# A SwiGLU kernel on one core: four rows per partition to a store, and sixty consecutive rows to each partition

## The chip, the core and the metric

The kernel runs on one core of a Trainium2 chip. The core has several engines with a queue of instructions each: VectorE (DVE), ScalarE (ACT), GpSimd (POOL) and SyncE (SP) are used here, TensorE is not. Sixteen DMA engines move data between DRAM and the on-chip memory, which has 128 partitions. Transfers are issued by SP, ACT or POOL; each of the three has a queue of its own on the DMA engines, and a transfer is done when its semaphore has been raised. The metric is the device time of one execution in microseconds (us). In the profile the transfers that SP issues are queue q1, those of ACT q10 and those of POOL q0.

## The reference

`x` is 8192 x 8192 in float32 (268 MB). Its left half is `a` and its right half `b`; the output is 8192 x 4096 (134 MB):

```python
a, b = np.split(x, 2, axis=-1)
silu_b = b / (1 + np.exp(-b))
return a * silu_b
```

Every element of `x` is read once and every element of the output is written once, 402.65 MB in all. One row of `x` is 32 KiB and one row of the output is 16 KiB.

## The kernel before

The rows are dealt out in 33 tiles. The first and the last tile have one row per partition (128 rows), the 31 between them two rows per partition (256 rows). Partition p of a two-row tile holds two neighbouring rows, so that a load moves 64 KiB in one piece to each partition and a store 32 KiB in one piece; the 128 pieces of a tile stand one behind the other in DRAM (L36 to L38, `in_dram`).

There are three buffers, the slots, of 64 KiB per partition, and tile i uses slot i modulo 3. For each tile `load` (L50) issues the load on SP. `swiglu` (L57) computes in the slot: ACT replaces `b` by silu(b) in place (L62), and DVE multiplies it by `a` and packs the products into the front of the same slot (L64). `store` (L73) sends that front part to DRAM. The two rows of a tile are one ACTIVATE and one multiplication of 128 x 8192 elements; tiles 1 and 31 are done in two pieces of one row (128 x 4096), and the first and last tile in two halves of a row (128 x 2048).

The program order is written out by hand at L83 to L97: three loads ahead, then for each tile compute, store, and the load that is to use the same slot. That load waits for the store (SP, L51), the store waits for the multiplication, the multiplication for the activation, and the activation for the load. Other waits between them are left out (`follows_from_others`), since they follow from these. Which engine issues a store is settled at L74 to L76: ACT, except for two stores in the middle of the kernel on POOL and the last three on SP. An engine's queue is worked off in order, so an instruction that waits holds up those behind it on the same engine.

Of the kernel before, what the change touches and what calls it, by code (L numbers as in the profile page):

```python
# [1 line left out]

# [4 lines left out]

_SILU = mybir.ActivationFunctionType.Silu


@with_exitstack
def kernel(
    ctx: ExitStack,
    tc: tile.TileContext,
    x: bass.AP,
    out: bass.AP,
):

    nc = tc.nc  # L20
    N, M = x.shape
    half = M // 2
    P = nc.NUM_PARTITIONS
    BUFS = 3

    rows = [1] + [2] * (N // P // 2 - 1) + [1]
    first = [sum(rows[:i]) * P for i in range(len(rows))]
    last = len(rows) - 1

    pool = ctx.enter_context(tc.tile_pool(name="sbuf", bufs=1))  # L30
    ctx.enter_context(tc.manual_schedule())
    slots = [pool.tile([P, 2 * M], x.dtype, name=f"slot{s}") for s in range(BUFS)]
    loads, gates, prods, stores = ([[] for _ in rows] for _ in range(4))
    newest = {}

    def in_dram(t, i, width):  # L36

        return bass.AP(t.tensor, first[i] * width, [[rows[i] * width, P], [1, rows[i] * width]])  # L38

    def follows_from_others(inst, i, current, earlier):  # L40


        targets = [t for kind in current for t in kind[i]]
        targets += [t for kind in earlier for j in range(i % BUFS, i, BUFS) for t in kind[j]]
        for t in targets:
            if t is not newest.get(inst.ins.engine):
                tc.declare_no_dep(inst.ins, t.ins, reason="ordered by the other waits")
        newest[inst.ins.engine] = inst

    def load(i):  # L50
        inst = nc.sync.dma_start(  # L51
            out=slots[i % BUFS][:, : rows[i] * M], in_=in_dram(x, i, M)
        )
        follows_from_others(inst, i, [], [loads, gates, prods])
        loads[i].append(inst)

    def swiglu(i, k0, k1, c0=0, cw=half):  # L57
        view = slots[i % BUFS].rearrange("p (k s c) -> p k s c", k=2, s=2)
        a = view[:, k0:k1, 0, c0 : c0 + cw]
        b = view[:, k0:k1, 1, c0 : c0 + cw]  # L60
        o = slots[i % BUFS][:, : 2 * half].rearrange("p (k c) -> p k c", k=2)
        gate = nc.scalar.activation(out=b, in_=b, func=_SILU)  # L62
        follows_from_others(gate, i, [], [loads, gates, prods, stores])
        prod = nc.vector.tensor_mul(out=o[:, k0:k1, c0 : c0 + cw], in0=a, in1=b)  # L64
        follows_from_others(prod, i, [loads], [loads, gates, prods, stores])
        gates[i].append(gate)
        prods[i].append(prod)

    def by_halves(i):
        for c0 in range(0, half, half // 2):  # L70
            swiglu(i, 0, 1, c0, half // 2)

    def store(i):  # L73
        eng = nc.scalar if i < last - 2 else nc.sync  # L74
        if i % 2 and last // 2 <= i < last // 2 + 4:
            eng = nc.gpsimd  # L76
        inst = eng.dma_start(  # L77
            out=in_dram(out, i, half), in_=slots[i % BUFS][:, : rows[i] * half]
        )
        follows_from_others(inst, i, [loads, gates], [loads, gates, prods, stores])  # L80
        stores[i].append(inst)

    for i in range(BUFS):  # L83
        load(i)
    for i in range(last):
        if i == 0:
            by_halves(i)
        elif i in (1, last - 1):
            swiglu(i, 0, 1)
            swiglu(i, 1, 2)  # L90
        else:
            swiglu(i, 0, rows[i])
        store(i)
        if i + BUFS <= last:
            load(i + BUFS)
    by_halves(last)
    store(last)  # L97


# [1 line left out]
_INS = ['x']  # L101
_OUTS = [((8192, 4096), 'float32')]


# [23 lines left out]
```

## Time and profile before

| | |
|---|---|
| median of three timed runs | 935.07 us (934.86 to 935.34) |
| profiled execution, first to last instruction | 933.16 us (the page rounds to 933.2) |
| around the span, against the median | 1.9 us |
| DVE busy | 278.7 us (30%), 37 instructions |
| ACT busy | 226.8 us (24%), 38 instructions |
| DMA packets | 9505, of which 1056 small ones that raise semaphores |
| HBM read and written | 268.44 MB and 134.22 MB, 431 GB/s over the span |
| loads, issue to landing (median) | 37.7 us |
| stores from ACT, issue to landing (median) | 33.5 us |

The profile is of one execution. Its page gives the busy time of each engine, the span in 40 slices with the busy share of the DMA engines in tenths, and the DMA queues with packets, bytes and the share of sixteen DMA engines that their packets took. The groups show instructions of one line and shape: count, busy time, mean duration in ns, the idle time before them and what ended it. A packet is one contiguous piece that one DMA engine moves: here the piece of one partition. The trace also keeps a record of each packet: its queue, size, start and duration.

### The profile page before, as it was taken

What the parts mean: (1) busy time and instruction counts of PE and PEld (TensorE: products, weight loads), DVE (VectorE), ACT (ScalarE), POOL (GpSimd) and SP (SyncE); (2) the same over time, 40 slices, a digit from 0 to 9 for tenths busy, and PEclk for the clock granted to TensorE, in tenths of its full rate; (3) what the DMA queues carried; (4) which work ended last, traced back from release to release, by engine and by line L of the source; (5) the groups of instructions that cost most, each with busy time, mean ns of one, the idle gap of its engine ahead of it and who ended that gap; (6) DMA issues with size and microseconds to landing.
All of it is one profiled execution on the core that took longest, in us unless ns stands there. A gap on an engine that the chain in (4) does not pass through costs nothing.

```text
span 933.2 us, 220 instructions
## 1 busy us (share of the span) xinstructions
DVE 278.7 (30%) x37; ACT 226.8 (24%) x38; POOL 1.4 (0%) x6
## 2 busy tenths in 40 slices
DVE  1312333123331233312333113332133321333242
ACT  2331133311333203332033320233202332023330
POOL 0000000000000000000000000000000000000000
DMA  9999999999999999999999999999999999999998
GB/s 405 405 449 431 423 451 444 409 444 433 444 427 434 442 410 448 428 433 442 434 421 441 445 417 444 428 454 427 420 457 405 449 427 428 448 445 409 427 444 388
DMA packets 9505, 402.67 MB, mean 432 GB/s; under 512 B 1056, under 2 KB 1056, under 8 KB 1056
## 3 DMA queue, kind: packets, MB, share of 16 engines
q1 hardware_dynamic: 5184, 278.92, 69.1%
q10 hardware_dynamic: 4032, 115.35, 28.6%
q0 software_dynamic: 288, 8.39, 2.1%
q14 instruction: 1, 0.01, 0.0%
HBM read 268.44 MB, written 134.22 MB: 431 GB/s over the span
## 4 chain that ended last, share of the span: by engine, by line
DMA 72%; DVE 11%; ACT 8%; issue 6%; another core or an unknown queue 1%; DVEq 0%; POOL 0%; SPq 0%; ACTq 0%; POOLq 0%
DMA slot<-in_x_dram 40%; DMA out_dram<-slot 32%; DVE slot L64 11%; ACT slot L62 8%; DVEq L123 0%; POOL out_dram L77 0%; SPq L51 0%; ACTq L77 0%; DVEq L64 0%; POOLq L123 0%
## 5 line engine op out<-in xcount | busy, mean ns | idle before, releaser
L64 DVE TENSOR_TENSOR slot<-slot 128x8192 f32<-128x8192 f32 (+2 forms) x37 | 278.7, 7539 | 636.7 <-ACT slot L62 636.5
L62 ACT ACTIVATE slot<-slot 128x8192 f32<-128x8192 f32 (+2 forms) x37 | 225.6, 6107 | 684.3 <-DMA slot<-in_x_dram 684.3
L77 POOL DMA_DIRECT2D out_dram<-slot x2 | 1.2, 600 | 568.9 <-DVE slot L64 568.9
L62 ACT ACT_TABLE_LOAD x1 | 1.3, 1283 | 0.7 <-PEq L112 0.7
L112 POOL MEMSET const-bfloat16-1.0<- 128x1 bf16 x1 | 0.1, 102 | 0.0
L112 POOL MEMSET const-float32-0.0<- 128x1 f32 x1 | 0.1, 99 | 0.2 <-issue 0.2
L112 POOL MEMSET const-float32-1.0<- 128x1 f32 x1 | 0.1, 99 | 0.0
L112 POOL MEMSET const-uint8-127<- 128x1 uint8 x1 | 0.1, 99 | 0.0
## 6 DMA issues: line engine op xcount, KB each, us to landing
out_dram<-slot ACTq DMA_DIRECT2D x27, 4096.0 KB, 33.5
slot<-in_x_dram SPq DMA_DIRECT2D x2, 4096.0 KB, 13.6
out_dram<-slot POOLq DMA_DIRECT2D x2, 4096.0 KB, 34.4
out_dram<-slot SPq DMA_DIRECT2D x2, 4096.0 KB, 20.4
out_dram<-slot ACTq DMA_DIRECT2D x1, 2048.0 KB, 28.1
out_dram<-slot SPq DMA_DIRECT2D x1, 2048.0 KB, 16.8
slot<-in_x_dram SPq DMA_DIRECT2D x31, 37.7
```

The source lines that it names most:

```text
L62: gate = nc.scalar.activation(out=b, in_=b, func=_SILU)
L64: prod = nc.vector.tensor_mul(out=o[:, k0:k1, c0 : c0 + cw], in0=a, in1=b)
L77: inst = eng.dma_start(out=in_dram(out, i, half), in_=slots[i % BUFS][:, : rows[i] * half])
L112: nc = _bacc.Bacc("TRN2", target_bir_lowering=False, num_devices=1)
```

## The change

The row order in DRAM and the use of the slots both change. The computation on each element does not.

The first 384 rows stay as they were: a one-row tile and a two-row tile. The last 128 rows stay a one-row tile too. The 7680 rows between them are divided among the partitions in 128 runs of 60 consecutive rows, and each partition works through its own run in 15 groups of four rows. `PITCH` is the distance of 60 rows between neighbouring partitions, which is 1,920 KiB in `x` and 960 KiB in the output.

A group of four rows is loaded by two loads of two rows, 64 KiB per partition each. The first, called A here, goes to a main slot (`mains`, two of the three slots, taken in turn), the second, called B, to the side slot (`side`, the third). A's rows are computed in place as before, two rows in one instruction of each engine. B's rows are computed one row at a time, and DVE writes their products not into the side slot but behind A's products in the main slot. The four rows of products then fill the main slot, 64 KiB per partition, and one store, called S, sends them. S of group g waits for the last product of the group.

The load A of group g+1 goes to the other main slot and waits for the store that frees it, that of group g-1. The load B of group g+1 waits for the last product of group g only, since the side slot is never stored from. On SP the order is A(g+1), B(g+1), A(g+2) and so on. The stores of groups 7, 8 and 9 are issued by POOL, the stores of group 14 and of the last one-row tile by SP, all others by ACT. The load of the last one-row tile stands behind B(14) on SP and waits for the store of group 13.

There are 33 loads as before, and 18 stores instead of 33. The core of the diff:

```diff
-    BUFS = 3
-
-    rows = [1] + [2] * (N // P // 2 - 1) + [1]
-    first = [sum(rows[:i]) * P for i in range(len(rows))]
-    last = len(rows) - 1
+    groups = (N // P - 4) // 4
+    PITCH = 4 * groups
...
-    slots = [pool.tile([P, 2 * M], x.dtype, name=f"slot{s}") for s in range(BUFS)]
+    slots = [pool.tile([P, 2 * M], x.dtype, name=f"slot{s}") for s in range(3)]
+    side, mains = slots[0], slots[1:]
...
+    def in_dram(t, start, step, rows, width):
+        return bass.AP(t.tensor, start * width, [[step * width, P], [1, rows * width]])
...
+    def swiglu(src, row, rows, dst, at, *needed, pieces=1):
+
+        view = src.rearrange("p (k s c) -> p k s c", k=2, s=2)
+        packed = dst.rearrange("p (k c) -> p k c", k=4)
+        last = None
+        for c0 in range(0, half, half // pieces):
+            cols = slice(c0, c0 + half // pieces)
+            a = view[:, row : row + rows, 0, cols]
+            b = view[:, row : row + rows, 1, cols]
+            gate = after(nc.scalar.activation(out=b, in_=b, func=_SILU), *needed)
+            last = after(
+                nc.vector.tensor_mul(out=packed[:, at : at + rows, cols], in0=a, in1=b), gate
+            )
+        return last
+
+    first = load(side, 0, 1, 1)
+    second = load(mains[0], P, 2, 2)
+    lead = [load(mains[1], 3 * P, PITCH, 2)]
+    base = 3 * P
+    firsts = {0: lead[0]}
+
+    done = swiglu(side, 0, 1, side, 0, first, pieces=2)
+    stored = store(nc.scalar, side, 0, 1, 1, done)
+    free_side = stored
+
+    def group(g):
+        return base + 4 * (g if PITCH != 4 else g * P)
+
+    seconds = {0: load(side, group(0) + 2, PITCH, 2, free_side)}
+    swiglu(mains[0], 0, 1, mains[0], 0, second)
+    done = swiglu(mains[0], 1, 1, mains[0], 1, second)
+    free = {0: store(nc.scalar, mains[0], P, 2, 2, done), 1: None}
+    last = None
+    for g in range(groups):
+        m = (g + 1) % 2
+        other = 1 - m
+        if g + 1 < groups:
+            firsts[g + 1] = load(mains[other], group(g + 1), PITCH, 2, free[other])
+        else:
+            last = load(mains[other], N - P, 1, 1, free[other])
+        swiglu(mains[m], 0, 2, mains[m], 0, firsts[g])
+        for k in range(2):
+            done = swiglu(side, k, 1, mains[m], 2 + k, seconds[g])
+        eng = nc.scalar if g + 1 < groups else nc.sync
+        if groups // 2 <= g < groups // 2 + 3:
+            eng = nc.gpsimd
+        free[m] = store(eng, mains[m], group(g), PITCH, 4, done)
+        if g + 1 < groups:
+            seconds[g + 1] = load(side, group(g + 1) + 2, PITCH, 2, done)
+    done = swiglu(mains[1 - m], 0, 1, mains[1 - m], 0, last, pieces=2)
+    store(nc.sync, mains[1 - m], N - P, 1, 1, done)
```

`load` issues on SP as before, `store` on the engine that it is given. The helper `after` takes the place of `follows_from_others`: it leaves to each instruction only the waits that are passed to it by name.

More of the change, by code (lines that the diff above doesn't have):

```diff
@@ L23 @@
     P = nc.NUM_PARTITIONS
-    BUFS = 3
-    rows = [1] + [2] * (N // P // 2 - 1) + [1]
-    first = [sum(rows[:i]) * P for i in range(len(rows))]
-    last = len(rows) - 1
+    groups = (N // P - 4) // 4
+    PITCH = 4 * groups
     pool = ctx.enter_context(tc.tile_pool(name="sbuf", bufs=1))
     ctx.enter_context(tc.manual_schedule())
-    slots = [pool.tile([P, 2 * M], x.dtype, name=f"slot{s}") for s in range(BUFS)]
-    loads, gates, prods, stores = ([[] for _ in rows] for _ in range(4))
+    slots = [pool.tile([P, 2 * M], x.dtype, name=f"slot{s}") for s in range(3)]
@@ L34, with after @@
+    side, mains = slots[0], slots[1:]
     newest = {}
[L36 to L46, printed above, removed]
+    def after(inst, *needed):
+        for t in (t for ts in everything for t in ts):
+            if t not in needed and t is not inst and t is not newest.get(inst.ins.engine):
@@ L47, in follows_from_others, with load @@
                 tc.declare_no_dep(inst.ins, t.ins, reason="ordered by the other waits")
         newest[inst.ins.engine] = inst
-    def load(i):
+        history.append(inst)
+        return inst
+    def in_dram(t, start, step, rows, width):
+        return bass.AP(t.tensor, start * width, [[step * width, P], [1, rows * width]])
+    history = []
+    everything = [history]
+    def load(slot, start, step, rows, *needed):
         inst = nc.sync.dma_start(
-            out=slots[i % BUFS][:, : rows[i] * M], in_=in_dram(x, i, M)
+            out=slot[:, : rows * M], in_=in_dram(x, start, step, rows, M)
@@ L53, in load @@
         )
[L54 to L75, printed above, removed]
-            eng = nc.gpsimd
[L77 to L97, printed above, removed]
+        return after(inst, *needed)
+    def store(eng, slot, start, step, rows, *needed):
+        inst = eng.dma_start(
+            out=in_dram(out, start, step, rows, half), in_=slot[:, : rows * half]
+        )
+        return after(inst, *needed)
@@ new lines, in swiglu @@
+    def swiglu(src, row, rows, dst, at, *needed, pieces=1):
[9 more added lines that the diff above has]
+                nc.vector.tensor_mul(out=packed[:, at : at + rows, cols], in0=a, in1=b), gate
+            )
+        return last
```

## The prediction

> **What bounds the kernel now.** I read the page's slices and DMA queues first, then the groups by form, the stretches at the end, and the waits of the queue of SP.
>
> ```profile
> DMA  9999999999999999999999999999999999999998
> GB/s 405 405 449 431 423 451 444 409 444 433 444 427 434 442 410 448 428 433 442 434 421 441 445 417 444 428 454 427 420 457 405 449 427 428 448 445 409 427 444 388
> DMA packets 9505, 402.67 MB, mean 432 GB/s; under 512 B 1056, under 2 KB 1056, under 8 KB 1056
> q1 hardware_dynamic: 5184, 278.92, 69.1%
> q10 hardware_dynamic: 4032, 115.35, 28.6%
> q0 software_dynamic: 288, 8.39, 2.1%
> ```
>
> The three queues add up to 99.8% of 16 DMA engines for the whole span: transfers bound the kernel from start to end, and no hole is left to fill. The engines are far behind:
>
> ```profile
> L64 DVE TENSOR_TENSOR slot<-slot 128x8192 f32<-128x8192 f32 x29 | 252.1, 8692 | 588.7 <-ACT slot L62 588.7
> L62 ACT ACTIVATE slot<-slot 128x8192 f32<-128x8192 f32 x29 | 203.9, 7031 | 633.6 <-DMA slot<-in_x_dram 633.6
> L64 DVE TENSOR_TENSOR slot<-slot 128x4096 f32<-128x4096 f32 x4 | 17.7, 4426 | 33.2 <-ACT slot L62 32.9
> L62 ACT ACTIVATE slot<-slot 128x4096 f32<-128x4096 f32 x4 | 14.2, 3609 | 37.1 <-DMA slot<-in_x_dram 37.1
> ```
>
> They idle two thirds of the time, waiting for loads. So only two things can move the time: what the DMA engines need for the same bytes, and whether they ever run dry. The stretches of the end (busy time and count per engine, clock, DMA share, GB/s) and its timeline show how close that is:
>
> ```profile
> 850.00:890.00 40.00, 17.39 (x2) 8.24 (x2) 0.00 (x0) 1.00 1.00 433
> 890.00:900.00 10.00, 0.00 (x0) 1.59 (x1) 0.00 (x0) 1.00 1.03 446
> 900.00:910.00 10.00, 7.84 (x2) 7.41 (x4) 0.00 (x0) 1.00 1.02 442
> 910.00:920.00 10.00, 5.42 (x3) 1.84 (x2) 0.00 (x0) 1.00 0.98 423
> ```
> ```profile
> 893.38 22.40 SPq L77 DMA_DIRECT2D out_dram<-slot  x3
> 898.41 7.12 ACT L62 ACTIVATE slot<-slot 128x4096 f32<-128x4096 f32 x2 [18.28 <-DMA slot<-in_x_dram]
> 902.06 13.36 DVE L64 TENSOR_TENSOR slot<-slot 128x4096 f32<-128x4096 f32 x4 [13.21 <-ACT slot L62]
> ```
>
> The last two-row load lands at 898.4 and its rows are multiplied by about 911.0 (902.06 + 2 × 4.43, and small hops), when its store can go. In those 12.6 us the DMA still holds the last one-row load and the store issued at 893.38, 4.19 MB each, 9.7 us each: 19.4 us of work. That is why the share stays near 1.00 there. The reader should keep this pair, work in the queue against time to the next issue, for the change.
>
> **The price of bytes and packets.** The trace's packet records (per queue and size) give it: all but a few 65,536-byte packets took 2,418 ns, 32,768 bytes 1,213, 16,384 bytes 611. The line through them is 8 ns per packet and 27.2 GB/s per engine, 435 GB/s for sixteen; each transfer ends with a 4-byte packet of 9 ns on each engine. Check: per engine before, 402.65 MB / 16 at 27.2 GB/s is 925.2 us, 528 packets × 8 ns 4.2, 66 transfers × 9 ns 0.6: 930.0, against first packet at 1.7 and last end at 931.9. So the records leave under a microsecond of idling.
>
> The records of one engine also show the order: a packet of one queue, then one of the other, whatever their sizes (S64 A32 S64 A32, 3.63 us a pair).
>
> **The change, part by part.**
>
> *Fewer, larger store packets.* Stores per partition: before 1 + 31 + 1 transfers, one packet each, 33 × 8 = 264 packets per DMA engine. After: 18 transfers (1 row, 2 rows, fifteen of 4, 1 row), 144 packets. Saved: 120 × 8 ns = 0.96 us, and 15 final packets × 9 ns = 0.13 us. Loads keep 33 transfers and 264 packets. Sum -1.1 us, all on the path, because the DMA is the path. The Trainium skill (DMA: Bandwidth & Descriptors, Anatomy of one DMA) prices each transfer at 2.0 us plus its bytes, which read as a cost in series would make 15 transfers fewer worth -30 us; the DMA share of 1.00 above speaks against it, since the fixed part lies under other transfers.
>
> *Smaller compute pieces.* The side slot's rows go one at a time: 30 pairs at 3.61 and 4.43 us in place of 15 at 7.03 and 8.69. ACT +0.19 × 15 = 2.9 us, DVE +0.17 × 15 = 2.5 us. Cost 0: hidden by the transfers, as the idle columns show. After the side load lands, 3.61 + 2 × 4.43 = 12.5 us pass until the group's store may go (one-piece form: 15.7).
>
> *Waits in the loop.* Call a group's loads A (into a main slot) and B (into the side slot), 8.39 MB each, its store S, 8.39 MB. A group is 25.2 MB, 58.1 us of DMA. SP issues A(g+1) when S(g-1) has landed, then B(g+1) when group g is multiplied, which is also when S(g) is issued. So S(g) and B(g+1) start together, but B queues behind what is left of A(g+1), and the two queues take turns packet by packet. With A(g+1) started when B(g) ended, 19.4 us long, and 12.5 us of compute plus about 1.3 of landing and issue gone, 5 to 6 us of A (2 to 3 packets per engine) are left. S therefore finishes that many packets ahead of B: 5 to 7 us, against about 1.3 us that A(g+2) needs to be issued and start. The DMA stays full; cost 0 per group, cover 4 to 5 us. If that cover were gone, up to 1.3 us a group. ACT waits with each store for DVE; behind it stands only the activation of A, not due for another 5 us. POOL issues three stores (0.53 and 0.67 us against 0.34 on ACT): hidden by the same remainder of A.
>
> *Start.* The first three loads and two stores have the same sizes and order as before; the next two loads wait for the same stores. Cost 0.
>
> *The end.* Here the pair shown above turns. After B(14), behind it on SP's queue, comes only the last one-row load, 4.19 MB: 9.7 us. S(13) is already done, by the 5 to 7 us just found. S(14) is issued when B(14)'s two rows are multiplied: landing x, 3.61 + 8.86 + about 0.1 of hops, 0.34 for the issue, y to the first byte. x + y: in the records 0.36 from final packet to landing and 0.63 from issue to first packet, and the mean DMA engine waits 0.3 for the slowest, together 1.3; the other end is the kernel's first load, issued at 0.74, used at 12.95: 12.21 less 0.37 issue and 9.64 for its bytes leaves 2.2. I take 1.3, nearer to a running queue; the first load's first packets were visibly slow. Hole: 12.91 + 1.3 - 9.7 = 4.5 us (4.2 to 5.4). All 16 DMA engines stand still in it. Afterwards S(14) and the last store (2.1 MB, issued before S(14) ends) run without a gap, as before.
>
> *Addresses.* Neighbouring partitions now read 1,920 KiB apart and write 960 KiB apart instead of 64 and 32. No row of this trace prices that: packets took the same time for loads and stores. I take 0. It can gain nothing, since the packet times follow size alone.
>
> **Sum.** -1.1 + 4.5 = +3.4 us (+3.1 to +4.3). The profiled span is 933.16, the measured median 935.07, 1.9 us around it. Forecast: 935.07 + 3.4 = **938.4 us** (0.4% slower); its own range, with half a microsecond for the timing, 937.6 to 940.
>
> **Rivals.**
>
> *The hole is covered (not slower).* If S(13) still had work when B(14) lands, this would fill the hole. It decides once S(13) has 1.5 us left there: of the net +3.4 less than 1.9 us then remains, which is 0.2%, about what a measurement of this kernel can tell from no change. In its full form the time is 935.07 - 1.1 = 934.0. For it: the turns by packet make S and B end within 7 us of each other, and an order in which B leads would do it. Against: the last load waits for S(13) itself, so a late S(13) opens its own 1.3 us gap, and before, the queue order held to the packet. 9%.
>
> *Holes in every group.* If the two take turns less evenly with 64 KiB on both sides, so that S ends after B, A(g+1) comes 1.3 us or more after the DMA ran dry, 14 times: +18, 956 us. Against: in the stores' records 32 and 64 KiB packets alternate one for one. 6%.
>
> *The wide spacing slows the packets.* If one packet in ten took the 3,052 ns that was the slowest record of a 64 KiB packet, the mean rises 2.6%, over 15 × 58.1 = 872 us: +23, 961 us. For it, the sixteen DMA engines would walk addresses at one fixed distance. Against: no record depends on place, and the distance is 15 × 128 KiB, no power of two. 9%. The Trainium skill (DMA: Bandwidth & Descriptors, Latency and other measured facts) reports copies with a row pitch of 2 MiB at 164 GB/s and of 512 KiB at 207, where 214 is full; by its mildest entry 3% would be lost, some +28 us by estimate. It speaks of large powers of two, which this pitch is not; no run here shows it.
>
> *The stores are not cut into 64 KiB packets.* Then the saving is 0.1 us and the time 939.4, in the forecast's range. 4%.
>
> The forecast has 70%. The range reaches from the half-covered hole (935.07 - 1.1 + 2.2 = 936.2) to 942, where a slight slowing of packets (0.4% of 872 us is 3.5) would end; beyond it lie the two large rivals, the full cover and a small remainder: near 2 in 10. Faster by over 0.2% would need -1.9 us, and everything that the trace lets me save is 1.1: 2%, for something that I do not see. Within 0.2%: the covered hole, 9%, and of the forecast's share 2% for a hole cut to less than 3 us: 11%. Slower: 68 + 6 + 9 + 4 = 87%.
>
> **What would show it.** In the profile after: packets for 128 × 18 stores, so 1,920 fewer of them and 240 fewer final ones; a DMA share of 1.00 until near 906 us, then a stretch of about 4.5 us in which it falls towards 0, just before the last four-row store, issued near 910 to 911; groups every 58.0 us on ACT; SP waiting for stores as before; no dips in the middle. I am wrong if the middle slices fall below 430 GB/s in the mean, or if the share near 907 to 911 stays near 1.00.

## The result, and the profile after

The changed kernel takes 975.05 us (median of four runs, 971.76 to 976.56), the kernel before 935.21 us beside it: the ratio is 1.0417 (95% interval 1.0404 to 1.0431). The forecast was 938.4 us with a range up to 942.0. The direction was right, the size was not: 40 us were lost instead of 3.4.

The lines of the page of the changed kernel that answer to those shown of before, the slices and the DMA queues with their packets, megabytes and shares:

```profile
DMA  9999998999999999999999999999999999999979
GB/s 389 430 432 432 427 392 351 432 432 427 432 395 432 411 411 432 432 438 422 395 432 419 432 395 419 419 416 435 422 403 432 405 435 411 413 406 433 432 311 389
DMA packets 7346, 402.67 MB, mean 415 GB/s; under 512 B 816, under 2 KB 816, under 8 KB 816
...
q1 hardware_dynamic: 5040, 278.92, 68.8%
q10 hardware_dynamic: 1872, 98.57, 23.5%
q0 software_dynamic: 432, 25.17, 6.0%
```

The packets are fewer as forecast: 2,160 fewer for the data and their final packets (and one more for instructions). But the shares still add up to 98.3% of a span that is 37 us longer. So most of the loss doesn't show as idle time. The DMA engines are recorded as busy and move fewer bytes: 415 GB/s in the mean against 432, with weak slices all along the span.

The packet records split it. Sum over sixteen DMA engines, divided by 16, with a packet's normal time taken from the size alone as in the prediction:

| us per DMA engine | before | after |
|---|---|---|
| normal time of the data packets | 929.7 | 928.7 |
| time of packets beyond their normal | 1.5 | 23.9 |
| time without a packet, between the first and the last | 0.7 | 15.8 |

The first row is the saving that was forecast, 1.0 us. The second row is the surprise: 272 of the 64 KiB load packets took over 3 us, against 8 before; store packets kept their normal time (0.3 us beyond it in sum). Of the third row, 4.2 us are the hole at the end, 5.5 us one hole near 144 us, and the rest small holes, most of them once in a group.

The hole at the end came as the prediction had it. The stretches around it (length, busy DVE, ACT and POOL with counts, clock, DMA share, GB/s) and the timeline of the end:

```profile
939.00:944.00 5.00, 4.42 (x2) 1.76 (x1) 0.00 (x0) 1.00 0.10 39
944.00:954.00 10.00, 4.49 (x2) 1.95 (x2) 0.00 (x0) 1.00 0.97 419
```
```profile
931.01 7.12 ACT L71 ACTIVATE slot<-slot 128x4096 f32<-128x4096 f32 x2 [26.95 <-DMA slot<-in_x_dram]
934.66 8.76 DVE L73 TENSOR_TENSOR slot<-slot 128x4096 f32<-128x4096 f32 x2 [21.87 <-ACT slot L71]
...
943.45 5.60 SPq L57 DMA_DIRECT2D out_dram<-slot  x2
```

B(14) is used from 931.0 on, the store of its group is issued at 943.45, and the share of the DMA is 0.10 in between, once the last one-row load is through.

The groups did not. One of them in the timeline: the issue of A(4), the use of B(3), the issue of S(3), and later the use of A(4) and of B(4).

```profile
267.42 59.92 SPq L51 DMA_DIRECT2D slot<-in_x_dram  x3
269.80 7.12 ACT L71 ACTIVATE slot<-slot 128x4096 f32<-128x4096 f32 x2 [27.12 <-DMA slot<-in_x_dram]
273.45 8.76 DVE L73 TENSOR_TENSOR slot<-slot 128x4096 f32<-128x4096 f32 x2 [22.05 <-ACT slot L71]
282.24 0.36 ACTq L57 DMA_DIRECT2D out_dram<-slot  x1
295.86 7.03 ACT L71 ACTIVATE slot<-slot 128x8192 f32<-128x8192 f32 x1 [18.94 <-DMA slot<-in_x_dram]
...
329.61 7.12 ACT L71 ACTIVATE slot<-slot 128x4096 f32<-128x4096 f32 x2 [26.72 <-DMA slot<-in_x_dram]
```

A is issued at 267.42, and B is already in use at 269.80. The prediction wanted 5 to 7 us between these two; they are 2.4 us apart. The records of one DMA engine (start in us, S64 a 64 KiB packet of the queue of SP, A64 one of the queue of ACT, sem a final packet) show what follows:

```
263.61:S64 266.02:S64 268.44:Ssem 268.45:S64 271.45:S64 273.87:S64 276.29:S64 278.70:S64
281.12:S64 283.54:S64 286.12:S64 290.19:A64 292.61:Ssem 292.61:A64 295.03:S64 297.44:A64
```

The first packet of A starts at 268.45 and takes 3.0 us; the packets after it take 2.42. The last one of A, just before the first packet of the store, takes 4.07 us. In the mean over the sixteen DMA engines this group lost 0.66 us in packets at the start of A, 1.24 us in those shortly before the first packet of S, and 0.3 us without a packet before A. From the store at 161.3 to that at 943.5 a group takes 60.2 us instead of 58.1.

### The profile page after: what moved, and what is told of

It is laid out like the page before. It is cut to its first block, busy times and chain, and to the rows that moved or that the text cites. A ratio compares the mean times of both kernels' runs of the same rounds, so it can differ in the third digit from the quotient of the medians.

```text
span 970.0 us, 238 instructions
## 1 busy us (share of the span) xinstructions
DVE 279.6 (29%) x51; ACT 228.1 (24%) x52; POOL 1.9 (0%) x7
## 4 chain that ended last, share of the span: by engine, by line
DMA 78%; DVE 13%; ACT 6%; DVEq 0%; issue 0%
DMA slot<-in_x_dram 71%; DVE slot L73 13%; DMA out_dram<-slot 8%; ACT slot L71 6%; DVEq L138 0%
## 5 line engine op out<-in xcount | busy, mean ns | idle before, releaser
L73 DVE TENSOR_TENSOR slot<-slot 128x4096 f32<-128x4096 f32 (+2 forms) x51 | 279.6, 5511 | 669.0 <-ACT slot L71 668.9
L71 ACT ACTIVATE slot<-slot 128x4096 f32<-128x4096 f32 (+2 forms) x51 | 226.8, 4481 | 717.1 <-DMA slot<-in_x_dram 717.1
```

The costliest lines, as they stand in the source:

```text
L71: gate = after(nc.scalar.activation(out=b, in_=b, func=_SILU), *needed)
L73: nc.vector.tensor_mul(out=packed[:, at : at + rows, cols], in0=a, in1=b), gate
```

## The experiments

**The spacing of the addresses, alone and undone.** The first change puts the four rows of neighbouring partitions side by side again; the second gives the kernel before the spacing of 60 rows and nothing else.

```diff
-    PITCH = 4 * groups
+    PITCH = 4
```
```diff
-        return bass.AP(t.tensor, first[i] * width, [[rows[i] * width, P], [1, rows[i] * width]])
+        start, step = first[i], rows[i]
+        if 2 <= i < last:
+            start, step = 3 * P + 2 * (i - 2), 60
+        return bass.AP(t.tensor, start * width, [[step * width, P], [1, rows[i] * width]])
```

> The changed kernel with one number changed back: four rows per partition stand side by side in DRAM again (PITCH = 4), slots, waits and packet sizes stay. Theory 1, the wide spacing slows load packets: the 64 KiB load packets return to 2.42 us throughout, the extra packet time of about 21 us and the lag of single DMA engines behind the others go, and what stays is the hole at the end: 938 to 941 us. Theory 2, the hand-over between store and load (both issued at the same instant, after one load has run alone) stretches packets and opens gaps whatever the addresses: 970 to 976 us, with load packets of over 3 us just before each store starts.

> The kernel before with the spacing alone: tiles 2 to 31 take two rows per partition at a pitch of 60 rows, everything else as before. Theory 1 (spacing slows packets): 64 KiB load packets longer than 2.42 us, 950 to 975 us. Theory 2 (hand-over): no change, 934 to 937 us.

Measured: 977.5 us without the spacing (ratio 1.0446, 1.0428 to 1.0463), 1.5 us above the range of theory 2, and 935.18 us in one run for the kernel before with it. The load packets beyond 3 us are 329 in the one and 12 in the other. Spacing is out, as cause and as help. The slices of the kernel before with the wide spacing are what its own were:

```profile
GB/s 404 404 449 430 424 449 444 410 449 425 442 430 442 428 416 448 428 438 437 440 416 444 431 428 448 428 449 424 433 440 417 444 427 433 444 438 416 438 435 385
```

**Two stores of 32 KiB per partition in place of one of 64.**

```diff
-        if groups // 2 <= g < groups // 2 + 3:
-            eng = nc.gpsimd
-        free[m] = store(eng, mains[m], group(g), PITCH, 4, done)
+        upper = eng.dma_start(
+            out=in_dram(out, group(g) + 2, PITCH, 2, half), in_=mains[m][:, 2 * half : 4 * half]
+        )
+        halves[g] = after(upper, done)
+        free[m] = store(eng, mains[m], group(g), PITCH, 2, done)
```

Load A waits for both of them.

> The changed kernel with each 64 KiB store as two of 32 KiB per partition, issued one behind the other by ACT (none by POOL); spacing and slots stay. With 32 KiB store packets against 64 KiB load packets the store takes 16 turns of 3.6 us, 58 us, so that it ends after the side load, and the next main load starts when the DMA is dry. Theory 1 (spacing): slow packets as in the changed kernel, plus a gap of 1 to 2 us a group: 975 to 995 us. Theory 2 (hand-over stretches packets because both sides have 64 KiB): slow packets go, gaps of 1 to 2 us a group stay: 955 to 968 us.

Measured: 986.87 us in one run. 323 load packets took over 3 us, and 31.5 us per DMA engine passed without a packet, 1.8 to 2.8 in nearly every group. So 64 KiB store packets are not what stretches the load packets, and theory 2 in the form of this run failed. The time falls into the range of theory 1, but the two runs before had already ruled that out. The run shows what they are good for in this scheme: at 32 KiB the store takes sixteen turns beside the loads, ends last, and every A comes into a dry DMA.

**B later by one multiplication.** VectorE squares a used row of the side slot and B waits for it; the squares are thrown away. This parts the issue of S from that of B by 4.4 us.

```diff
+            used = side[:, :half]
+            later = after(nc.vector.tensor_mul(out=used, in0=used, in1=used), done)
-            seconds[g + 1] = load(side, group(g + 1) + 2, PITCH, 2, done)
+            seconds[g + 1] = load(side, group(g + 1) + 2, PITCH, 2, later)
```

> The changed kernel, but the side load B is issued 4.4 us after the store S instead of in the same instant: VectorE first squares one used row of the side slot in place (its values are thrown away) and the load waits for that. Theory 2a, two transfers issued at the same instant stretch the packets in flight: the load packets of over 3 us just before each store vanish, about 1.2 us a group, 17 us in all, 950 to 960 us. Theory 2b, the stretch belongs to a store queue starting beside a load queue that holds one nearly finished load: it stays, 968 to 978 us.

Measured: 970.8 us in one run, 311 load packets over 3 us. The issue of two transfers in one instant is not the cause. But a third theory came out of these four traces. In a few groups of the changed kernel (the stores at 100.8, 223.5 and 403.6 us) nothing was stretched, neither at the start of A nor before S. In just these A had been issued 5 us or more before B landed (5.3 to 6.6 us). Where A's first packet had its normal time, so had the packet before S, though S and B were issued in one instant there too. So both delays would belong to one event: A arriving when its queue is dry or nearly so.

**All stores on the queue of the loads.** Then S, B and the next A stand one behind the other, and A is issued 19 us ahead of its turn. The second kernel also stores the last group in two halves; `early` is the multiplication of its A rows.

```diff
-        eng = nc.scalar if g + 1 < groups else nc.sync
-        if groups // 2 <= g < groups // 2 + 3:
-            eng = nc.gpsimd
+        eng = nc.sync
```
```diff
+        if g + 1 == groups:
+            store(nc.sync, mains[m], group(g), PITCH, 2, early)
...
+            inst = nc.sync.dma_start(
+                out=in_dram(out, group(g) + 2, PITCH, 2, half), in_=mains[m][:, 2 * half : 4 * half]
+            )
```

> The changed kernel with all stores of four rows issued by SP, on the queue of the loads, so that S and B run one behind the other and the next A is queued 19 us ahead of its turn. Theory 2b (two queues meeting): no stretched packets and no gaps but the one at the end: 937 to 940 us. If appending transfers to a queue that holds one nearly finished load is what stretches packets, the stretch stays at about 1.2 us a group: 953 to 960 us.

> As the run before, and in addition the last four-row group is stored in two halves, the two rows of its A load as soon as they are multiplied, so that 4.19 MB of store stand in the queue while the last side rows are multiplied. If the hole at the end is what the prediction said, 4.5 us go: with no stretch 933.5 to 935 us, which would be 0.1% faster than the kernel before; with the stretch 949 to 955 us.

Measured: 941.6 us in one run, and 940.82 us with the early half of the last store (ratio 1.0048, 1.0031 to 1.0064; 937.49 to 944.15). The loss in the groups is gone: in the first, 10 packets of 64 KiB over 3 us, and outside the end only 0.3 us without a packet. Its slices:

```profile
GB/s 402 407 441 446 446 402 446 446 424 424 446 427 421 446 435 435 424 441 435 424 432 438 444 416 438 444 430 421 444 444 413 441 444 432 419 444 444 424 310 402
```

The first kernel is 1.6 us above its expected range; its hole at the end is 5.8 us in the records. The second missed its 933.5 to 935 us. On the DMA engine whose records I read, the packets follow each other through the end without a gap; but one DMA engine was by then 5.4 us behind the first, so the others stood still and waited (4.4 us in the mean). I take it that in a single queue that is never dry nothing makes the engines wait for each other, so that small delays add up; that is argued, not tested. In the one-queue run before it the spread grew from 0.4 to 2.7 us.

**B later by three multiplications, and the early store with it.** Here S and B stay on two queues, as in the change.

```diff
+            used = side[:, :half]
+            for _ in range(3):
+                later = after(nc.vector.tensor_mul(out=used, in0=used, in1=used), done)
-            seconds[g + 1] = load(side, group(g + 1) + 2, PITCH, 2, done)
+            seconds[g + 1] = load(side, group(g + 1) + 2, PITCH, 2, later)
```

> The changed kernel with the side load B issued 13.3 us after the store S (three squarings of a used row on VectorE, thrown away, stand between). S then has the DMA almost to itself at first and ends 7 to 10 us ahead of B, so that the next main load A is queued long before its turn. Theory 3, the one cause of the lost time in the groups is that A arrives when its queue is dry or nearly so: no gaps, no load packets over 3 us at the start of A, and none before S either; only the hole at the end stays: 937 to 941 us. Theory 2b, a store queue that starts beside a load queue stretches packets by itself: the 1.2 us a group stay: 953 to 960 us.

> As the run before, and the last four-row group is stored in two halves, the first as soon as the rows of its A load are multiplied. If theory 3 holds and the hole at the end is 4.5 us for want of queued work, this gives 933.8 to 936 us, level with the kernel before or 0.1% faster.

Measured: 940.75 us (ratio 1.0056, 1.0041 to 1.0072) and, with the early half store, 936.55 us (ratio 1.0014, 1.0005 to 1.0023). Adding 186 us of useless work to VectorE made the changed kernel 34 us faster. The slices and groups of the first of the two, with the squarings on L112:

```profile
GB/s 402 422 427 447 447 402 447 433 416 444 441 438 416 441 444 416 441 438 444 416 436 444 422 436 441 441 419 438 441 422 436 441 441 419 438 441 422 436 318 402
...
L112 DVE TENSOR_TENSOR slot<-slot 128x4096 f32<-128x4096 f32 x42 | 185.7, 4422 | 1.0
```

And a group in its timeline, with S at 274.43, B at 287.68 and the next A 22.7 us after that:

```profile
274.32 13.33 DVE L112 TENSOR_TENSOR slot<-slot 128x4096 f32<-128x4096 f32 x3
274.43 0.34 ACTq L57 DMA_DIRECT2D out_dram<-slot  x1
286.21 7.03 ACT L71 ACTIVATE slot<-slot 128x8192 f32<-128x8192 f32 x1 [17.10 <-DMA slot<-in_x_dram]
287.68 23.02 SPq L51 DMA_DIRECT2D slot<-in_x_dram  x2
```

A is issued 9.6 to 9.7 us before B lands in every group. Before the end no slice is below 402 GB/s, where the kernel before has 405 as its lowest; a group takes 58.05 us (from 157.6 to 912.3, thirteen groups), and the delays at A and S are under 0.1 us in each. What remains is the hole at the end. The early store closes it; the end of the first kernel, then that of the second:

```profile
906.00:912.00 6.00, 6.00 (x2) 3.42 (x3) 0.00 (x0) 1.00 0.15 66
```
```profile
905.00:912.00 7.00, 7.00 (x2) 4.42 (x3) 0.00 (x0) 1.00 0.98 421
```

So the hole is worth 4.2 us in time. In the records of the first kernel it is 5.5 us in the mean, but the engines come out of it level, and without it they end 2.0 us apart. The second kernel is still 1.5 us slower than the kernel before, and 0.6 us above its expected range: its DMA engines are 2.0 us apart at the end (0.6 before), its packets took 2.4 us beyond their normal time (1.5 before), and the saved 1.0 us doesn't pay for that.

**A late on purpose, in one queue.** In the one-queue version VectorE writes a product of eight columns of B's landed rows into the slot of the next A, and A waits for it. The products of A's rows are moved ahead of this, and those of B's rows wait for them; the last one-row load is made late in the same way.

```diff
+        prod_a = swiglu(mains[m], 0, 2, mains[m], 0, firsts[g])
+        mark = mains[other][:, :8]
+        tail_of_b = side[:, M : M + 8]
+        late = after(
+            nc.vector.tensor_mul(out=mark, in0=tail_of_b, in1=tail_of_b), seconds[g], free[other]
+        )
...
-            firsts[g + 1] = load(mains[other], group(g + 1), PITCH, 2, free[other])
+            firsts[g + 1] = load(mains[other], group(g + 1), PITCH, 2, late)
...
-        swiglu(mains[m], 0, 2, mains[m], 0, firsts[g])
...
+            done = swiglu(side, k, 1, mains[m], 2 + k, seconds[g], behind=(prod_a,))
```

> The one-queue version (all stores on SP, measured at 941.6 us) with A made late on purpose: VectorE multiplies eight columns out of B's landed rows into the slot that A is to fill, and A waits for it, so A is issued when B has landed and the DMA is dry. Theory 3: a gap of 1.3 to 2.5 us and a stretched first packet (0.6 us) in each of 14 groups, and S after it stretches packets too (1.2 us): 980 to 1000 us. If the stretch before S needs two queues, only gap and first packet: 965 to 985 us, with no long packets before S.

Measured: 997.61 us in one run, 56 us more than the one-queue version. A group in its timeline, from the use of B (210.64) to the issue of the next A (210.91) and of S (223.08), and the next S:

```profile
210.64 7.12 ACT L71 ACTIVATE slot<-slot 128x4096 f32<-128x4096 f32 x2 [31.71 <-DMA slot<-in_x_dram]
210.71 0.17 DVE L102 TENSOR_TENSOR slot<-slot 128x8 f32<-128x8 f32 x1 [23.06 <-DMA slot<-in_x_dram]
210.91 0.33 SPq L51 DMA_DIRECT2D slot<-in_x_dram  x1
...
223.08 0.34 SPq L57 DMA_DIRECT2D out_dram<-slot  x1
...
285.17 0.34 SPq L57 DMA_DIRECT2D out_dram<-slot  x1
```

A group takes 62.1 us. In nearly every group there are 2.0 to 2.4 us without a packet, 0.6 to 0.7 us in the first packet of A, and 1.1 to 1.35 us in the last packets of A before S: 58 + 2.2 + 0.7 + 1.2 = 62.1. A late A is enough for both delays, and S needs no queue of its own for the second.

**How early is early enough.** The first kernel has two squarings (8.9 us). The second has none; it computes the side rows in halves of a row, which brings S forward instead.

```diff
-            for _ in range(3):
+            for _ in range(2):
```
```diff
-            done = swiglu(side, k, 1, mains[m], 2 + k, seconds[g])
+            done = swiglu(side, k, 1, mains[m], 2 + k, seconds[g], pieces=2)
```

> As the run with B issued 13.3 us after S, but with two squarings, 8.9 us. With none S lands about 2.5 us before B, with one (4.4 us) about 5 us, and both lost the 30 us; with three about 10 us, and nothing was lost. Theory 3 with the time an issue takes to reach the DMA engines (1 us, and two packets of 2.4 us already chosen) needs about 6 us: this run, at 7 to 8 us, should be whole: 939 to 943 us. If more is needed, 955 to 972 us.

> The changed kernel with the side rows computed in halves of a row, which brings the store S 1.7 us earlier after B has landed (1.9 + 4 x 2.29 us against 3.6 + 2 x 4.43). No work is added or thrown away. Theory 3: S lands 1 to 2 us earlier ahead of B than in the changed kernel, 4 us in all, which is still under the 6 us that are needed: 962 to 974 us. If the threshold is lower than I think: 940 to 955 us.

Measured, in one run each: 942.11 us and 953.81 us, with 936.36 us for the kernel before beside them. The first is whole. Its margin, from the issue of A to the landing of B, is 4.8 or 4.9 us in every group, not the 7 to 8 us that I expected; so the time came out in its range though the margin didn't. The delays are 0.4 us or less. The second did better than I expected, because less margin is needed than 6 us.

How much is needed, the landing of B doesn't tell well, for it is that of the slowest DMA engine. The third column therefore has the margin on the DMA engines themselves, from the issue of A to the end of B's last packet on each, in the mean of the sixteen:

| kernel | margin to the landing, us | margin on the engines, us | packet delay in the 24 us after A's issue, us per DMA engine |
|---|---|---|---|
| as changed | 2.4 to 4.8, eleven groups | -0.2 to 2.6 | 0.8 to 2.0 |
| as changed | 5.3 and 5.8 | 4.4 and 3.7 | 0.03 and 0.01 |
| side rows in halves | 3.4 to 4.4, seven groups | 1.6 to 2.5 | 1.1 to 1.9 |
| side rows in halves | 4.8 to 5.0, six groups | 2.9 to 3.4 | 0.03 to 0.3 |
| side rows in halves | 4.8, one group | 2.3 | 1.7 |
| B 4.4 us later | 2.3 to 5.3, all | -0.2 to 2.4 | 1.1 to 2.1 |
| changed, without the spacing | -0.2 to 6.5, twelve groups | -4.8 to 2.5 | 1.3 to 2.0 |
| changed, without the spacing | 4.8, two groups | 3.0 and 3.6 | 0.10 and 0.04 |
| B 8.9 us later | 4.8 to 4.9, all | 3.0 to 4.1 | 0.0 to 0.4 |
| B 13.3 us later | 9.6 to 9.7, all | 7.8 to 8.1 | 0.05 or less |

The fourteenth group of the changed kernel, not in the table, is the one with the long hole below (-4.6 us, 1.9 us of delay). By the landing the groups don't part: with 4.8 us some are whole and some are not, and one with 6.5 us lost 1.3. By the margin on the engines all 84 groups of these six kernels do (A(2) to A(14) and the last one-row load of each): those with 2.6 us or less lost 0.8 us or more, those with 2.9 us or more lost 0.4 or less. One 64 KiB packet takes 2.42 us, so A has to be issued a little more than one packet before the DMA engines run out of B.

## Why the prediction was wrong

**The saving** was right: the normal packet time fell by 1.0 us, with 0.13 us of final packets outside that figure, against the 1.1 of the sum. The Trainium skill (DMA: Bandwidth & Descriptors, Anatomy of one DMA) fits its 2.0 us to transfers issued by GpSimd, as only three of the 18 stores here are; read as a cost in series of every transfer it would have given 30 us for 15 fewer, and these are in no run here.

**The hole at the end** was right in its place in the chain, in cause and in size: 4.2 us in the records against 4.5, and 4.2 us between the two kernels that differ in it.

**Smaller pieces, start, addresses** cost nothing, as forecast: the pieces kept 3.61 and 4.42 us, and the wide spacing alone gave 935.18 us. The rival of the spacing, at 9%, is refuted. The Trainium skill (DMA: Bandwidth & Descriptors, Latency and other measured facts) reports losses for row pitches at large powers of two; 1,920 KiB is no power of two, and this run shows no loss at it.

**The step that failed is "Waits in the loop".** It gave the groups a cost of 0, with S 5 to 7 us ahead of B against 1.3 us that A needs. Both numbers were wrong.

The first left out what lies between the issue of S and its first packet. The prediction let S take its turns as soon as it was issued. In the kernel before, the rows already showed otherwise: the store issued at 76.63 has its first packet at 80.58 in the records, 3.9 us later. About 1.0 of that is the way of an issue to a DMA engine with nothing to do (in the run with A late, 210.91 to 211.87), which leaves more than the 2.42 us of one load packet. In the changed kernel it is 4.6 to 7.3 us, in the mean of the engines, for the stores of groups 0 to 13. With that, A has one packet left or none, not two or three, when S begins. Measured: in eleven groups of fourteen A was issued 2.4 to 4.8 us before B landed, and on the DMA engines 2.6 us or less before B's last packet ended.

The second took the issue time for the need. Issued 1.3 us ahead, A would be there when the queue runs dry; the packets stayed whole only where it was issued 2.9 us or more ahead on the DMA engines. That this and the late start of S are one thing, the engines settling more than one packet in advance, fits both figures but isn't shown.

And the price of a miss was mis-sized. The rival "holes in every group" took 1.3 us of dry DMA as all of it: 18 us. The dry time itself was 0.1 to 1.5 us in the groups with a late A, besides the long hole, but behind it came packet delays of about 1.9 us in most (0.2 to 1.1 at the start of A, 0.9 to 1.7 before S), which no part of the prediction knew of, and the drifting apart of the DMA engines. From store to store a group took 2.1 us more than the 58.1 forecast. The sum in the changed kernel: 23.9 - 1.5 = 22.4 us of packet delays, 5.5 us in the hole at 144 us, some 5 us of short holes, 4.2 us at the end, less the saving of 1.0: 36 us, against 36.8 us between the two spans.

The long hole is a case of its own. In the stretch of 6 us the DMA stands almost still:

```profile
144.00:150.00 6.00, 0.00 (x0) 1.10 (x1) 0.00 (x0) 1.00 0.05 22
```

Two of the sixteen DMA engines had taken 0.1 to 1.0 us more for many of their packets between 107 and 143 us and came in with S(0) and B(1) 5 us after the others. A(2) waits for S(0), so fourteen DMA engines waited for two. The run without the spacing had two such holes, of 5.9 and 6.4 us. Why two DMA engines slow down together in some runs stays open.

I said that I would be wrong if the middle slices fell below 430 GB/s in the mean; they did.

## What to carry to other kernels

When one DMA queue's next transfer waits for the end of another's, count the margin from its issue to the moment when its queue runs dry, and count it in packets and on each DMA engine, not by the landing of the slowest: here a little more than one packet was needed (2.6 us were too little, 2.9 enough, with 64 KiB packets of 2.42 us). A transfer that comes later costs more than the gap that one sees, so look at the durations of packets, not only at the busy share, which stayed above 98% here. In a kernel whose DMA was full from start to end, a change that saves 1 us of packets and makes the chain of waits shorter by one slot has little to win and the overlap to lose.

## What the runs showed of the hardware that was not expected

- A load that came to a dry or nearly dry queue had 0.1 to 1.2 us more in its first packets, in the mean of the DMA engines, and the load packets just before the next store's first packet took 0.6 to 1.7 us more, these on all sixteen in nearly every such group; with the load issued 2.9 us or more before its queue ran dry both together were 0.4 us at most, and 0.1 or less in most groups. It happened with S on a queue of its own and on that of the loads, with 64 and 32 KiB store packets, at 1,920 and 128 KiB of spacing. What delays the second packet, some 15 to 18 us after the dry moment, stays open.
- The sixteen DMA engines drift apart: to 2.7 and to 5.4 us towards the end of two runs with one queue, against 0.6 at the end of the kernel before. The landing of a transfer is that of the slowest.
- Spacing the partitions' rows 1,920 KiB apart in place of 64 changed no packet time: 935.18 us, with 0.9 us of delay in 64 KiB packets against 0.8.
